# Gate and branch projections of a hybrid block written token-major, with a transpose of the merged result

## Chip, cores and metric

One core of one Trainium2 chip. The metric is the device time of one execution in microseconds, that of the only core; three runs of a kernel are made and their median is given.

## The reference

Two layers of a mixer and a feed-forward net on 256 tokens of width 1024, all in float32. Cut to what the change touches:

```python
proj = x @ w_in
gq, gk, gv, gg, glr, gz, mq, mk, mv, gl = jnp.split(proj, offsets, axis=-1)
a = gla_branch(gq, gk, gv, gg, glr, w_gate_up, b_gate, gla_norm_w) @ w_branch[0]
b = gmlp_branch(gz, gmlp_ln_g, gmlp_ln_b, gmlp_w_s, gmlp_b_s) @ w_branch[1]
c = moba_branch(mq, mk, mv, positions) @ w_branch[2]
ga, gb, gc = jnp.split(jax.nn.sigmoid(gl), N_BRANCH, axis=-1)
return (ga * a + gb * b + gc * c) @ w_out
```

`gl` has 3 x 1024 columns (the gates), each `w_branch` is 512 x 1024, `w_out` is 1024 x 1024. After it come a residual and a layer norm, then `square(relu(x @ w_ff1)) @ w_ff2` with 4096 hidden columns and a second layer norm.

## The kernel before

**Products.** A float32 product is made of three products of rounded operands: with x = hi + lo, each weight is split into `whi` (ScalarE, `split_hi`, L115) and `wlo` (VectorE, `split_lo`, L120), each activation likewise, and TensorE adds hi·hi, hi·lo and lo·hi in a PSUM bank. There are three ways to do so:

- `acc_s` (L281): the activation (128 tokens) is the stationary operand and the weight moves, three matmuls for each block of 128 inputs; with 512 weight columns that is 3 x 512 moving columns, and the result is token-major (tokens on the partitions).
- `acc_wide` (L265): the weight (128 columns) is stationary and the tokens move. One matmul with 512 moving columns takes `whi` against hi and lo side by side, one with 256 takes `wlo` against hi. The result is channel-major, in two halves of a bank that `fold` (L277) adds with a ScalarE copy and a VectorE add.
- `acc_w` (L255): the same with three matmuls of 256 moving columns, no fold.

A product of 1024 columns with all 256 tokens has the same number of moving columns in each of the three.

**Order of the work.** The program is a list of units (`add_unit`): each has TensorE work on one or two pieces of weight (512 KB each, loaded by the SyncE queue, SP), and often a `post` that empties its banks. The loop at L1061 goes through the units; at each it first advances the generators in `side` by one step (`advance`), then puts out the splits due there (`splits`), then the unit's matmuls, then its `post`. Pieces are split up to 7 units ahead (`LEAD`), in 9 buffers; the raw pieces go through 4 buffers (and 6 more early on), and a load is issued when `take_lo` has freed its buffer. All five queues work in this order; what an engine waits for holds up all that is behind it there. The PSUM banks are two rings of four, `pw` and `ps`.

**Units of a layer.** First `v` and `gv` (in layer 0 by `first_units`, L589: one piece of k = 0 for `v`, one for `gv`, then pieces of both for k = 1 to 7; the activations come in four pieces, split by `split_x` when the first unit that needs them is prepared), `u`, `gg`, the gates of branch b (`post_gl(1)`), the product of branch b (`branch_units`, L769, by `acc_w`), gk, gq, mq, mk, mv, the gates of a and c between the small matmuls of the attention (`moba_main`), the products of branches a and c, `w_out`, the layer norm, and the feed-forward units. Gates, u, gk, gq, mq, mk and `ff1` go through `acc_wide`; v, gv, gg, mv, `w_out` and `ff2` through `acc_s`.

**Gates and merge.** `gates` is one tile of 24 blocks of 128 channels x 256 tokens. `post_gl` folds a block; a later step applies the sigmoid in place. `post_bb`, `post_ba`, `post_bc` multiply a branch's block in its bank with its gate (VectorE); `post_ba` and `post_bc` add up the three on GpSimd (L815, L825). Since the sum is channel-major it is at once the stationary operand of `w_out`: `split` (L827) makes its hi (ScalarE) and lo (VectorE), block by block. `transpose_split` (L211), with four 128x128 transposes on TensorE, a ScalarE copy and a VectorE subtraction, turns token-major data and is used behind the layer norms.

Of the kernel before, what the change touches and what calls it, by code (L numbers as in the profile page):

```python
# [9 lines left out]
F32 = mybir.dt.float32  # L10
# [11 lines left out]
NT = 2  # L22
# [32 lines left out]
def block_kernel(ctx, tc, ins, out):  # L55
# [247 lines left out]
    def build_layer(l, xT):  # L303
# [285 lines left out]
        def first_units():  # L589

            blocks = [(0, piece(w_in[:, 0:1, C_V:C_V + 512], 1, 512)), (0, piece(w_in[:, 0:1, C_GV:C_GV + 512], 1, 512))]
            blocks += [(k, piece(w_in[:, k:k + 1, C_V:C_V + 1024], 1, 1024)) for k in range(1, 8)]
            heads = {0: 0, 2: 1, 3: 2, 5: 3}
            for n, (k, p) in enumerate(blocks):
# [3 lines left out]
                def pe(k=k, p=p, n=n):  # L598
                    for i, nm in enumerate(("v", "gv")):
                        if n < 2 and i != n:  # L600
                            continue
                        c0 = i * 512 if n > 1 else 0
# [6 lines left out]
                    for i, nm in enumerate(("v", "gv")):  # L609
                        if n < 2 and i != n:  # L610
                            continue
                        c0 = i * 512 if n > 1 else 0
# [135 lines left out]
        def post_gl(br):  # L748
            def post(m, p):
                if "G" not in st:  # L750
                    st["G"] = v3(sbt("G", 6144, "gates"), 24)
                G = st["G"]
                i = br * 8 + m
                fold(G[:, i], p)
                raw = st.setdefault("raw", [])
                raw.append(i)
                if m % 2 and (br == 1 or st.get("exps_done")):
                    def act():
                        while raw:
                            a = raw.pop(0)  # L760
                            nc.scalar.activation(G[:, a], G[:, a], AF.Sigmoid)
                        yield
                    side.append(act())
            return post

        st["glb_unit"] = len(units)
        w_units(C_GL + 1024, 8, post_gl(1))

        def branch_units(br, key, post):  # L769
            wb = ins["w_branch"][l][br].rearrange("(k p) c -> p k c", p=128)  # L770
            for j in range(4):
                b = w_pieces(wb, j * 256, 256, 4)[0]

                def pe(b=b, j=j):
                    for i in range(2):
                        st["pb", br, 2 * j + i] = pbank("pw", "pB")
                        acc_w(st["pb", br, 2 * j + i][:, :256], b, st[key], slice(i * 128, (i + 1) * 128), 0, True, True)

                def po(j=j):
                    for i in range(2):  # L780
                        post(2 * j + i, st["pb", br, 2 * j + i][:, :256])
                add_unit([b], pe, po)

        def post_bb(m, p):
            g = st["G"][:, 8 + m]
# [20 lines left out]
        w_units(C_GL, 8, post_gl(0))  # L806
        units[first_gl].start = lambda: side.append(moba_main())
        w_units(C_GL + 2048, 8, post_gl(2))


        def post_ba(m, p):
            G = st["G"]
            g = G[:, m]
            nc.vector.tensor_tensor(g, p, g, op=OP.mult)
            nc.gpsimd.tensor_tensor(G[:, 8 + m], G[:, 8 + m], g, op=OP.add)  # L815
# [4 lines left out]
        def post_bc(m, p):  # L820
            G = st["G"]
# [292 lines left out]
```

## Time and profile before

| | us |
|---|---|
| median of three runs (872.25 to 872.44) | 872.27 |
| the profiled execution | 872.83 |
| its span | 871.1 |
| TensorE (PE) matmuls busy | 860.2 (99%) |
| weight loads (PEld) busy | 751.4 (86%) |
| VectorE (DVE) busy | 617.7 (71%) |
| ScalarE (ACT) busy | 468.0 (54%) |
| GpSimd (POOL) busy | 59.5 (7%) |

Busy times are a share of the span; the profiled execution takes 1.7 us more than its span. A matmul's own duration overlaps that of the next, so what one costs is read from the distance between the starts of two, or from a run of many in the chain of work that ended last.

### The profile page before, as it was taken

How to read it: one execution, taken by the hardware profiler on the slowest of the kernel's cores; microseconds unless marked ns; L12 is line 12 of the kernel's file. 1: busy time of each engine (PE TensorE's matmuls, PEld its weight loads, DVE VectorE, ACT ScalarE, POOL GpSimd, SP SyncE). 2: the span in 40 equal slices, each digit the busy share in tenths (PEclk: the TensorE clock that was granted, in tenths of full speed). 3: DMA queues.
4: the chain of work that ended last, by engine and by line, in shares of the span. 5: the costliest groups of instructions: out<-in, count | busy, mean ns of one | idle time of the engine just before them, and what ended most of it. 6: DMA issues, size and time to landing. Idle time of an engine off the chain costs nothing.

```text
span 871.1 us, 13093 instructions
## 1 busy us (share of the span) xinstructions
PE 860.2 (99%) x5020; PEld 751.4 (86%) x5020; DVE 617.7 (71%) x949; ACT 468.0 (54%) x768; POOL 59.5 (7%) x73
## 2 busy tenths in 40 slices
PE   9999999999999999999999999999999999999996
PEld 7898887889989888888889898878898988888885
DVE  6779798666796666666777767958667856666665
ACT  6657663567445544445454756645744555444440
POOL 0010000102400000000000100010042000000001
PEclk9999999999999999999999999999999999999999
DMA  9577665346566655556655765544467465555531
GB/s 324 201 220 214 198 218 151 115 148 191 189 198 212 217 190 186 190 191 209 216 172 170 218 198 165 171 120 146 151 217 229 147 224 193 193 194 194 194 121 48
DMA packets 118718, 162.10 MB, mean 186 GB/s; under 512 B 5472, under 2 KB 100480, under 8 KB 118656
## 3 DMA queue, kind: packets, MB, share of 16 engines
q1 hardware_dynamic: 118512, 161.15, 57.8%
q8 instruction: 39, 0.64, 0.3%
q14 instruction: 23, 0.19, 0.1%
q10 hardware_dynamic: 144, 0.13, 0.0%
HBM read 160.21 MB, written 1.05 MB: 185 GB/s over the span
## 4 chain that ended last, share of the span: by engine, by line
PE 92%; DVE 3%; DMA 2%; ACT 1%; issue 1%; SPq 0%; DVEq 0%; ACTq 0%
PE acc L287 25%; PE pW L275 25%; PE pF L275 17%; PE pB L263 8%; PE pF L287 4%; PE pSmv L287 3%; DVE wlo L120 1%; PE pGG L287 1%; PE pSgv L287 1%; PE pSv L287 1%; PE pkv L457 1%; DMA xraw<-in_xT_dram 1%; DMA inv<-in_rope_inv_dram 1%; PE po L481 1%; PE pT L214 1%
## 5 line engine op out<-in xcount | busy, mean ns | idle before, releaser
L115 ACT CAST whi<-wraw 128x1024 fp32r<-128x1024 f32 (+1 forms) x281 | 283.3, 1039 | 132.2 <-DMA wraw<-in_w_ff_dram 63.2
L120 DVE TENSOR_TENSOR wlo<-wraw,whi 128x1024 fp32r<-128x1024 f32 (+1 forms) x281 | 334.7, 1226 | 18.1 <-ACT whi L115 17.8
L275 PE MATMUL pW<-actT,whi 128*128 128x512 f32 x704 | 248.3, 401 | 0.0
L275 PE MATMUL pW<-actT,wlo 128*128 128x256 f32 x704 | 183.3, 281 | 0.0
L287 PE MATMUL acc<-whi,h 128*128 128x512 f32 x512 | 163.4, 391 | 0.0
L275 PEld LDWEIGHTS pW<-actT,whi 128*128 128x128 f32 x704 | 128.1, 188 | 24.4
L275 PE MATMUL pF<-actT,whi 128*128 128x512 f32 x416 | 146.7, 397 | 0.0
L275 PEld LDWEIGHTS pW<-actT,wlo 128*128 128x128 f32 x704 | 132.9, 189 | 7.3 <-DVE wlo L120 0.2
L287 PEld LDWEIGHTS acc<-whi,h 128*128 128x128 f32 x512 | 96.2, 188 | 19.0
L275 PE MATMUL pF<-actT,wlo 128*128 128x256 f32 x416 | 108.4, 281 | 0.0
L287 PE MATMUL acc<-wlo,h 128*128 128x512 f32 x256 | 99.8, 390 | 0.0
L279 DVE TENSOR_TENSOR fr<-pF,fr 128x256 f32<-128x256 f32 x52 | 21.9, 424 | 102.0 <-ACT fr L278 102.0
L275 PEld LDWEIGHTS pF<-actT,whi 128*128 128x128 f32 x416 | 76.5, 188 | 15.4
L275 PEld LDWEIGHTS pF<-actT,wlo 128*128 128x128 f32 x416 | 78.5, 189 | 4.4
L287 PEld LDWEIGHTS acc<-wlo,h 128*128 128x128 f32 x256 | 48.1, 188 | 10.0
L278 ACT COPY fr<-pF 128x256 f32<-128x256 f32 x52 | 19.1, 372 | 59.4 <-PE pF L275 59.4
L209 POOL TENSOR_TENSOR mvar<-mvar,halfc 128x1 f32<-128x1 f32 x12 | 10.8, 904 | 443.1 <-DVE mvar L208 443.1
L287 PE MATMUL acc<-whi,actT 128*128 128x512 f32 x128 | 40.3, 391 | 0.0
L287 PE MATMUL pF<-whi,actT 128*128 128x256 f32 x192 | 36.6, 287 | 0.0
L279 DVE TENSOR_TENSOR gates<-pW,gates 128x256 f32<-128x256 f32 x48 | 19.5, 421 | 17.8 <-ACT gates L278 17.4
L278 ACT COPY gates<-pW 128x256 f32<-128x256 f32 x48 | 16.9, 370 | 27.3 <-PE pW L275 27.3
L946 ACT CAST h<-fr 128x256 fp32r<-128x256 f32 x52 | 19.3, 407 | 21.5 <-DVE fr L945 21.5
(234 smaller groups left out, 1238.6 us busy)
## 6 DMA issues: line engine op xcount, KB each, us to landing
wraw<-in_w_ff_dram SPq DMA_DIRECT2D x128, 512.0 KB, 4.9
wraw<-in_w_in_dram SPq DMA_DIRECT2D x104, 512.0 KB, 4.3
wraw<-in_w_branch_dram SPq DMA_DIRECT2D x24, 512.0 KB, 4.3
wraw<-in_w_out_dram SPq DMA_DIRECT2D x16, 512.0 KB, 3.3
wearly<-in_w_in_dram SPq DMA_DIRECT2D x7, 512.0 KB, 9.4
wraw<-in_w_in_dram SPq DMA_DIRECT2D x6, 396.0 KB, 4.4
lng<-in_ln_g_dram SPq DMA_DIRECT2D x4, 512.0 KB, 5.4
lnb<-in_ln_b_dram SPq DMA_DIRECT2D x4, 512.0 KB, 7.3
```

The source lines that it names most:

```text
L115: nc.scalar.copy(p.hi, p.raw)
L120: nc.vector.tensor_tensor(p.lo, p.raw, p.hi.bitcast(F32), op=OP.subtract)
L209: nc.gpsimd.tensor_tensor(dst, dst, half_c.to_broadcast([128, n]) if n > 1 else half_c, op=OP.pow)
L214: nc.tensor.transpose(p[:, k * 128:(k + 1) * 128], src[:, (half * 4 + k) * 128:(half * 4 + k + 1) * 128], ident)
L263: nc.tensor.matmul(o, w, a, start=start and i == 0 and j == 0, stop=stop and i == n - 1 and j == 2)
L275: nc.tensor.matmul(d, w, a, start=start and i == 0 and j == 0, stop=last and j == 1)
L278: nc.scalar.copy(dst, p[:, 256:])
L279: nc.vector.tensor_tensor(dst, p[:, :256], dst, op=OP.add)
L287: nc.tensor.matmul(o, a, w, start=start and j == 0, stop=stop and j == 2)
L457: nc.tensor.matmul(p[:, h * 128:(h + 1) * 128], kT4[rows, t, h, :], v4[rows, t, h, :], start=True, stop=True)
L481: nc.tensor.matmul(p[r, c], at4[:, t, h, r], v4[:, t, h, :], start=first and r.start == 0, stop=True)
L946: nc.scalar.copy(hi[:, i], rr[i])
```

## The change

Four edits:

1. **Gates** (`gl_units`, `half_units`): by `acc_s`, token-major, in two halves of 512 columns, each four units with one piece of two k (512 columns). The `post` of a half puts the sigmoid from the bank straight into `gates` for 128 x 512 at a time; the gates of a, which are ready before the exponentials of the attention are done, are copied first and get their sigmoid later. There is no fold.
2. **Branch products and merge** (`branch_units`): by `half_units` too, two units for each half, products on 128 x 512. The last addition is on VectorE, that of a stays on GpSimd. The sum is token-major and has to be turned: `turn` calls `transpose_split` for each token tile and half, two steps of `advance` after its `post`.
3. **`acc_wide`**: instead of wide and narrow in turn, all wide matmuls of a unit's k together and all narrow ones together (wide first, but narrow first in the unit that closes the bank). This holds for u, gk, gq, mq, mk and `ff1`, which stay channel-major.
4. **`first_units`**: the pieces of k = 1 for `v` and `gv` are apart, as those of k = 0 were, with 512 columns each, in the order v of k = 0 and 1, gv of k = 0 and 1. There is one unit more, the parameters' load moves from unit 3 to unit 5.

```diff
-        for i in range(n):
-            k = k0 + i
-            tr = [(o, p.hi[:, i, cs], both[:, k, :]), (o[:, :256], p.lo[:, i, cs], hi[:, k, :])]
-            last = stop and i == n - 1
-            for j, (d, w, a) in enumerate(tr[::-1] if last else tr):
-                nc.tensor.matmul(d, w, a, start=start and i == 0 and j == 0, stop=last and j == 1)
+        wide = [(o, p.hi[:, i, cs], both[:, k0 + i, :]) for i in range(n)]
+        narrow = [(o[:, :256], p.lo[:, i, cs], hi[:, k0 + i, :]) for i in range(n)]
+        tr = narrow + wide if stop else wide + narrow
+        for j, (d, w, a) in enumerate(tr):
+            nc.tensor.matmul(d, w, a, start=start and j == 0, stop=stop and j == len(tr) - 1)
...
-            blocks = [(0, piece(w_in[:, 0:1, C_V:C_V + 512], 1, 512)), (0, piece(w_in[:, 0:1, C_GV:C_GV + 512], 1, 512))]
-            blocks += [(k, piece(w_in[:, k:k + 1, C_V:C_V + 1024], 1, 1024)) for k in range(1, 8)]
-            heads = {0: 0, 2: 1, 3: 2, 5: 3}
+            blocks = [(k, piece(w_in[:, k:k + 1, c:c + 512], 1, 512)) for c in (C_V, C_GV) for k in (0, 1)]
+            blocks += [(k, piece(w_in[:, k:k + 1, C_V:C_V + 1024], 1, 1024)) for k in range(2, 8)]
+            heads = {0: 0, 1: 1, 4: 2, 6: 3}
...
+        def half_units(src, kt, xk, post):
+
+            for hf in range(2):
+                for k0 in range(0, kt, 2):
+                    b = piece(src(k0, hf * 512), 2, 512)
+
+                    def pe(b=b, k0=k0, hf=hf):
+                        x = xk()
+                        for t in range(NT):
+                            if k0 == 0:
+                                st["phalf", hf, t] = pbank("pw", "pH")
+                            for i in range(2):
+                                acc_s(st["phalf", hf, t], b, i, x, k0 + i, t, slice(0, 512), k0 + i == 0, k0 + i == kt - 1)
+
+                    def po(hf=hf):
+                        for t in range(NT):
+                            post(t, slice(hf * 512, (hf + 1) * 512), st["phalf", hf, t])
+                    add_unit([b], pe, po if k0 == kt - 2 else None)
...
+            def post(t, sl, p):
+                g = gates(br, t)[:, sl]
+                if br == 1 or st.get("exps_done"):
+                    nc.scalar.activation(g, p, AF.Sigmoid)
+                else:
+                    nc.scalar.copy(g, p)
+                    st.setdefault("raw", []).append(g)
...
-        def post_bc(m, p):
-            G = st["G"]
-            g = G[:, 16 + m]
-            hi, lo, _ = mT()
-            nc.vector.tensor_tensor(g, p, g, op=OP.mult)
-            nc.gpsimd.tensor_tensor(g, g, G[:, 8 + m], op=OP.add)
-
-            def split():
-                nc.scalar.copy(hi[:, m], g)
-                nc.vector.tensor_tensor(lo[:, m], g, hi[:, m].bitcast(F32), op=OP.subtract)
-                yield
-            side.append(split())
+        def post_bc(t, sl, p):
+            g = gates(2, t)[:, sl]
+            nc.vector.tensor_tensor(g, p, g, op=OP.mult)
+            nc.vector.tensor_tensor(g, g, gates(1, t)[:, sl], op=OP.add)
+
+            def turn():
+                yield
+                hi, lo, _ = mT()
+                transpose_split(gates(2, t), hi, lo, t, sl.start // 512)
+                yield
+            side.append(turn())
...
-    units[3].start = sts[0]["params"]
+    units[5].start = sts[0]["params"]
...
-    for n, c in ((0, 0), (2, 1), (3, 2), (5, 3)):
+    for n, c in ((0, 0), (1, 1), (4, 2), (6, 3)):
         load_more(n)
         load_xT(c)
```

**Where the order changes.** TensorE at the end of branch c (`pB` and `pH` are its banks, `ch` and `cl` the branch's hi and lo, `acc` the banks of `w_out`); before:

```order
L263 MATMUL pB<-ch,whi 128x256
L263 MATMUL pB<-cl,whi 128x256
L263 MATMUL pB<-ch,wlo 128x256
L287 MATMUL acc_2507<-whi,actT 128x512
L287 MATMUL acc_2507<-wlo,actT 128x512
L287 MATMUL acc_2507<-whi,actT 128x512
```

and in the change, ahead of the branch's last unit:

```order
L286 MATMUL pH<-whi,cl 128x512
L214 MATMUL pT<-ident,gates 128x128 x8
L286 MATMUL pH<-whi,ch 128x512
L286 MATMUL pH<-wlo,ch 128x512
L286 MATMUL pH<-whi,cl 128x512
```

and behind the first unit of `w_out`:

```order
L286 MATMUL acc_2172<-wlo,actT 128x512
L286 MATMUL acc_2172<-whi,actT 128x512
L214 MATMUL pT<-ident,gates 128x128 x8
L286 MATMUL acc_2201<-whi,actT 128x512
L286 MATMUL acc_2201<-wlo,actT 128x512
L286 MATMUL acc_2201<-whi,actT 128x512
```

Eight transposes stand ahead of the branch's last unit, and eight behind the first unit (12 matmuls) of `w_out`.

VectorE at the same place (`wlo` are the splits of coming weights); before, two of the four rounds of branch c:

```order
L120 TENSOR_TENSOR wlo<-wraw,whi 128x1024
L824 TENSOR_TENSOR gates<-pB,gates 128x256 x2
L829 TENSOR_TENSOR actT<-gates,actT 128x256 x2
L120 TENSOR_TENSOR wlo<-wraw,whi 128x1024
L824 TENSOR_TENSOR gates<-pB,gates 128x256 x2
L829 TENSOR_TENSOR actT<-gates,actT 128x256 x2
```

and in the change, both halves:

```order
L835 TENSOR_TENSOR gates<-pH,gates 128x512
L836 TENSOR_TENSOR gates<-gates 128x512
L835 TENSOR_TENSOR gates<-pH,gates 128x512
L836 TENSOR_TENSOR gates<-gates 128x512
L120 TENSOR_TENSOR wlo<-wraw,whi 128x1024 x2
L217 TENSOR_TENSOR actT<-pT,actT 128x4x128 x2
L120 TENSOR_TENSOR wlo<-wraw,whi 128x1024
L835 TENSOR_TENSOR gates<-pH,gates 128x512
L836 TENSOR_TENSOR gates<-gates 128x512
L835 TENSOR_TENSOR gates<-pH,gates 128x512
L836 TENSOR_TENSOR gates<-gates 128x512
L120 TENSOR_TENSOR wlo<-wraw,whi 128x1024
```

The products and sums of the second half stand behind the lo of the first half's turn (L217) and one split.

TensorE in the first units of u (`acc_wide`); before:

```order
L275 MATMUL pW<-actT,whi 128x512
L275 MATMUL pW<-actT,wlo 128x256
L275 MATMUL pW<-actT,whi 128x512
L275 MATMUL pW<-actT,wlo 128x256
L275 MATMUL pW<-actT,whi 128x512
L275 MATMUL pW<-actT,wlo 128x256
```

and in the change:

```order
L274 MATMUL pW<-actT,whi 128x512 x4
L274 MATMUL pW<-actT,wlo 128x256 x4
L274 MATMUL pW<-actT,whi 128x512 x4
L274 MATMUL pW<-actT,wlo 128x256 x8
L274 MATMUL pW<-actT,whi 128x512 x4
L274 MATMUL pW<-actT,wlo 128x256 x4
L274 MATMUL pW<-actT,whi 128x512 x8
```

The turns from narrow to wide become fewer: three in a round of 16 pairs.

## Rows read from the trace of the kernel before

**Rows 1.** Page, parts 1 and 2: busy time and share, and the clock in 40 slices.

```profile
span 871.1 us, 13093 instructions
...
PE 860.2 (99%) x5020; PEld 751.4 (86%) x5020; DVE 617.7 (71%) x949; ACT 468.0 (54%) x768; POOL 59.5 (7%) x73
...
PEclk9999999999999999999999999999999999999999
```

**Rows 2.** Waits of TensorE, the whole program: total us, times, longest.

```profile
PE pSv L614 <- DVE wlo L120: 1.1, 1, 1.1
...
PE plr L740 <- DVE gates L279: 0.8, 1, 0.8
```

**Rows 3.** Chain that ended last, TensorE's pieces: start us, us, instructions in a row.

```profile
95.57 28.16 PE pW L275 x160
...
209.47 23.02 PE pB L263 x192
...
280.15 5.63 PE pF L275 x32
285.78 5.44 PE acc L287 x24
...
432.27 0.87 PE pT L214 x8
...
441.34 1.01 PE pT L214 x8
...
447.83 5.44 PE pSv L287 x24
```

**Rows 4.** Timeline of TensorE, from branch c to w_out: start us, us, instruction.

```profile
232.21 0.28 PE L263 MATMUL pB<-ch,wlo 128*128 128x256 f32 x1
232.33 0.40 PE L287 MATMUL acc<-whi,actT 128*128 128x512 f32 x1
232.56 0.40 PE L287 MATMUL acc<-wlo,actT 128*128 128x512 f32 x1
...
233.49 0.62 PE L287 MATMUL acc<-whi,actT 128*128 128x512 f32 x2
```

**Rows 5.** Timeline of TensorE, layer 0's first matmuls.

```profile
5.89 0.63 PE L607 MATMUL pSv<-whi,actT 128*128 128x512 f32 x1
6.32 0.63 PE L608 MATMUL pSv<-whi,actT 128*128 128x512 f32 x1
...
10.41 0.39 PE L608 MATMUL pSgv<-whi,actT 128*128 128x512 f32 x1
11.87 0.73 PE L614 MATMUL pSv<-wlo,actT 128*128 128x512 f32 x2 [1.07 <-DVE wlo L120]
...
12.90 0.40 PE L607 MATMUL pSv<-whi,actT 128*128 128x512 f32 x1
```

**Rows 6.** Timeline of VectorE and ScalarE, layer 0's start.

```profile
9.99 0.69 DVE L984 TENSOR_TENSOR actT<-xraw,actT 128x512 fp32r<-128x512 f32 x1 [3.38 <-ACT actT L983]
10.59 2.42 DVE L120 TENSOR_TENSOR wlo<-wearly,whi 128x1024 fp32r<-128x1024 f32 x2
...
10.71 1.04 ACT L115 CAST whi<-wearly 128x1024 fp32r<-128x1024 f32 x1 [0.76 <-DMA wearly<-in_w_in_dram]
```

**Rows 7.** Timeline of TensorE, end of branch b's gates in layer 0.

```profile
73.63 0.28 PE L275 MATMUL pW<-actT,wlo 128*128 128x256 f32 x1
74.74 0.39 PE L740 MATMUL plr<-ident,lrs 128*16 128x128 f32 x2 [0.82 <-DVE gates L279]
```

**Rows 8.** VectorE's groups of instructions: shape and count | busy us, mean ns.

```profile
L120 DVE TENSOR_TENSOR wlo<-wraw,whi 128x1024 fp32r<-128x1024 f32 x272 | 327.0, 1237 | 18.1 <-ACT whi L115 17.8
...
L228 DVE SCALAR_TENSOR_TENSOR xr<-xr,acc 128x512 f32<-128x512 f32 x16 | 11.0, 686 | 11.8 <-PE acc L287 11.8
```

**Rows 9.** ScalarE's groups of instructions.

```profile
L115 ACT CAST whi<-wraw 128x1024 fp32r<-128x1024 f32 x272 | 276.7, 1048 | 131.7 <-DMA wraw<-in_w_ff_dram 63.2 <-DMA wraw<-in_w_in_dram 37.3 <-PE acc L287 11.9
```

**Rows 10.** Page, part 6: a load of w_out, us from issue to landing.

```profile
wraw<-in_w_out_dram SPq DMA_DIRECT2D x16, 512.0 KB, 3.3
```

More of the change, by code (lines that the diff above doesn't have):

```diff
@@ L599, in pe @@
                     for i, nm in enumerate(("v", "gv")):
-                        if n < 2 and i != n:
+                        if n < 4 and i != n // 2:
                             continue
-                        c0 = i * 512 if n > 1 else 0
+                        c0 = i * 512 if n > 3 else 0
                         for t in range(NT):
@@ L609, in pe @@
                     for i, nm in enumerate(("v", "gv")):
-                        if n < 2 and i != n:
+                        if n < 4 and i != n // 2:
                             continue
-                        c0 = i * 512 if n > 1 else 0
+                        c0 = i * 512 if n > 3 else 0
                         for t in range(NT):
@@ L746, in build_layer, with gates @@
         gg_units()
[L748 to L751, printed above, removed]
-                G = st["G"]
[L753 to L757, printed above, removed]
+        def gates(br, t):
+            if "G" not in st:
+                st["G"] = v3(sbt("G", 6144, "gates"), 6)
+            return st["G"][:, br * 2 + t]
@@ L758, in act, with gl_units @@
+        def gl_units(br):
+            c = C_GL + br * 1024
+            def post(t, sl, p):
[5 more added lines that the diff above has]
+                    st.setdefault("raw", []).append(g)
+                if t == 1 and st.get("raw") and st.get("exps_done"):
                     def act():
-                        while raw:
-                            a = raw.pop(0)
-                            nc.scalar.activation(G[:, a], G[:, a], AF.Sigmoid)
@@ L762, in act @@
-                        yield
+                        while st["raw"]:
+                            a = st["raw"].pop(0)
+                            nc.scalar.activation(a, a, AF.Sigmoid)
+                            yield
                     side.append(act())
-            return post
+            half_units(lambda k, c0: w_in[:, k:k + 2, c + c0:c + c0 + 512], 8, xT, post)
         st["glb_unit"] = len(units)
-        w_units(C_GL + 1024, 8, post_gl(1))
+        gl_units(1)
         def branch_units(br, key, post):
@@ L770, in branch_units @@
             wb = ins["w_branch"][l][br].rearrange("(k p) c -> p k c", p=128)
[L771 to L782, printed above, removed]
@@ L784, in post_bb @@
-        def post_bb(m, p):
-            g = st["G"][:, 8 + m]
+            half_units(lambda k, c0: wb[:, k:k + 2, c0:c0 + 512], 4, lambda: st[key], post)
+        def post_bb(t, sl, p):
+            g = gates(1, t)[:, sl]
             nc.vector.tensor_tensor(g, p, g, op=OP.mult)
@@ L1016, in block_kernel @@
         free = max(q.last for q in pieces[:n - SPLIT_BUFS + 1]) + 1 if n >= SPLIT_BUFS else -LEAD
-        s = max(prev + 1, free, p.first - (LEAD if n > 8 else 1))
+        s = max(prev + 1, free, p.first - (LEAD if n > 9 else 1))
         if count < 2 and max(prev, free) == prev and (p.first - s < 3 or p.first - s < LEAD - 1 and prev >= extra + 2):
@@ L1022, in block_kernel @@
         hi_at.setdefault(max(s, -1), []).append(p)
-        lo_at.setdefault(max(min(s + 1, p.first), s, -1) if n > 8 else max(s, -1), []).append(p)
+        lo_at.setdefault(max(min(s + 1, p.first), s, -1) if n > 9 else max(s, -1), []).append(p)
     loaded = [0]
```

13 lines of the change are left out of this document (6 added, 7 removed).

## The prediction

> **What bounds the kernel now.** I read the page's busy shares first, then the waits of TensorE, then the chain of work that ended last, and last the timeline where TensorE stands still. The reader is to see that TensorE's queue is the program's clock: PE is busy for 860.2 of 871.1 us, at a granted clock that the page prints as 9 (the 2.4 GHz level) in all 40 slices [rows 1]; behind its warm-up it waited for another engine only twice, 1.1 us for the low half of a weight in layer 0's start and 0.8 us at `plr` [rows 2]. VectorE (71%) and ScalarE (54%) are nowhere the bound for long [rows 1]. So an edit is worth what it takes out of TensorE's stream, plus those two waits, less new ones.
>
> A matmul's own duration says nothing here, since it overlaps with the next. The chain gives the pace [rows 3]: with 512 columns in `acc_s`, 24 in 5.44 us, 0.2267 us each (v, and `ff2` the same); with 256 in `acc_w`, 192 in 23.02 us, 0.1199 each; a pair of `acc_wide` (512 and 256 in turn), 80 in 28.16 us, 0.352 each, and 16 in 5.63 in `ff1`. A wide and two narrow ones have the same columns, but 2 x 0.1199 is 0.240 against 0.2267; a pair has one and a half times the columns of a wide one, and 1.5 x 0.2267 is 0.340 against 0.352. The stream pays for each matmul and not only for its columns.
>
> **Gates.** A layer has 3 x 8 blocks x 8 k = 192 pairs, the program 384: 135.2 us. In `acc_s` it is 3 branches x 2 halves x 2 token tiles x 8 k x 3 = 288 wide matmuls a layer, 576 in all: 130.6 us. **-4.6.** The small matmuls of the attention that lie between stay as they are.
>
> **Branch products.** 288 narrow ones a layer, 576 in all: 69.1 us; then 144 wide ones a layer, 288 in all: 65.3 us. **-3.8.** Both terms lie on the path whole, since TensorE is the path.
>
> [...]
>
> **Grouping.** What stays in `acc_wide` is 20 blocks x 8 k (u, gk, gq, mq, mk) and 208 pairs of `ff1` a layer, 736 pairs, 46 rounds of 16. A round takes 5.63 us; pure runs of either kind would make it 16 x 0.3466 = 5.55. So at most 0.08 us a round, 3.9 us in all, can be won. What a return from narrow to wide costs stands where branch c ends: the first five intervals of wide ones, 232.33 to 233.49, take 1.16 us where 5 x 0.2267 is 1.13 [rows 4], some 0.03 for one return behind a long narrow run. The new order has three returns a round: at 0.03 each nothing would be won. Blocks of four are shorter than those five intervals and I take half, 0.016 a return, 0.05 a round: **-1.6**, bounds 0 and -3.9.
>
> **Transposes.** Two layers x two halves x eight. Eight of them behind a layer norm take 0.87 us of the chain, once 1.01 [rows 3]: **+3.5**, up to 4.0. They could wait, too. For the second half VectorE has to do, behind the branch's last matmul, product and sum of the last tile, about 0.69 us each by the nearest row of this size [rows 8], 1.4 us; the cover is a `w_out` unit of 12 matmuls, 2.72 us. Ahead of that in its queue stand one split (1.24 us) and two lo of the first half's turn [rows 8], 2.6 us that can start 2.7 us earlier, when those transposes are out. It fits with about nothing to spare, so I put the wait at 0, with 0.6 us for each of the four as bound. What is queued behind waiting transposes is all of `w_out`; the banks behind the turn (ScalarE's hi, VectorE's lo) are wanted only two units later, 5.4 us.
>
> **First pieces.** TensorE's start 10.41 is followed by one at 11.87: 1.46 us where 0.23 is due [rows 5]. The cause is the order on VectorE: it splits the activations of k = 2 and 3 (9.99, when they had landed) ahead of the weights of k = 1 (10.59) [rows 6]. In the change the four small lo come first, so this wait goes. What is late next is k = 2: its weight's hi was made from 10.71 to 11.75 [rows 6], and TensorE began it at 12.90 [rows 5]. So 1.15 us at most; one load more now stands on SP's queue ahead of this weight, and I take **-0.9**, bounds 0 and -1.15. The parameters of the layer norm in the gMLP are asked for one piece later; they are wanted by VectorE alone, while TensorE has u ahead of it.
>
> **The wait at `plr`.** 73.63 to 74.74 is 1.11 us for a narrow matmul (0.12) [rows 7]: the next bank of the ring held a gate block whose fold was late on VectorE. With four banks for a whole branch's gates the bank in question was emptied by a sigmoid units before: **-1.0**, bounds 0 and -1.0.
>
> **At nothing:** the folds of the gates (gone), the sigmoids (now from the bank), the last additions (from GpSimd to VectorE), the loads of 2 x 512 instead of 4 x 256: all beside a TensorE that doesn't wait for them. If that cover went, it would be through the turn, below. There are as many weight pieces as before, but for one in the head.
>
> **Sum:** -4.6 - 3.8 - 1.6 + 3.5 - 0.9 - 1.0 = -8.4 us. The profiled execution took 872.83, so 864.4 for it; the median lies 0.56 lower, 872.27, and so I forecast **863.9**. What a measurement of this kernel can tell from no change is 0.2%, 1.74 us.
>
> **Rivals.**
> *The small terms fail:* grouping and head give nothing, `plr` waits for something else, the turns wait 0.6 us each: -8.4 + 1.6 + 0.9 + 1.0 + 2.4 + 0.5 = -2.0, at worst 870.3, still faster. For it: each rests on one or two rows. 14%.
> *Columns alone:* the pace goes with the columns, and the surplus of narrow ones is their surroundings'. Then gates, branches and grouping give nothing, and +3.5 - 0.9 - 1.0 = +1.6 makes 873.9, no change. Against it: 192 narrow ones in a row at 0.1199 and wide ones at 0.2267 in two places [rows 3]. 5%. [...]
> *The turn waits (slower):* VectorE works in order. If a split ahead of the second half's products waits for its weight of `w_out`, then load (3.3 us [rows 10]), hi (1.05 [rows 9]) and lo (1.24 [rows 8]) come before the transposes, and TensorE behind them stands still for up to 5.6 us a layer: 863.9 + 11.2 = 875.1. It decides from (8.4 + 1.7) / 2 = 5.1 us a layer. For it: ScalarE's casts do wait for loads (idle time before them in [rows 9]). Against it: splits run units ahead. 5%.
> *The clock falls (slower):* in the first microseconds 512 columns took 0.43 us (5.89 to 6.32), the pace of the 1.2 GHz level, though later 0.227 [rows 5]. If each of the four groups of transposes brought that back for the time it lasted at the start, some 6 us at half speed or 3 us each, 863.9 + 12 = 875.9. The Trainium skill says that transposes don't count as busy for the clock (TensorE: Matmul & The Clock Gate, Part 4: PE-mode transpose). Against it: behind the transposes at 441.34 wide matmuls go on at 0.2267 [rows 3], and no slice shows less than 9 [rows 1]. 3%.
>
> **How the numbers follow.** The forecast with its terms inside their bounds has 73%, from 872.27 - (4.6 + 3.8 + 3.9 - 3.5 + 1.15 + 1.0) = 861.3 to about 866.5. With better than half of the small-terms case, up to 868.5, that is 8 in 10: range 861.4 to 868.5. Faster by over 0.2%: 73 + 14 = 87%; within 0.2%: 5%; slower: 5 + 3 = 8%.
>
> **What would show it.** In the changed kernel's chain: `pH` matmuls at 0.2267 (a run of 24 in 5.44 us) in gates and branches; a round of 32 in `ff1` of 5.58 to 5.60 instead of 5.63; eight transposes of `gates` in some 0.87 us, twice a layer; no wait of TensorE at `plr`; k = 2 begun at about 12.0. It would be wrong if TensorE waited for VectorE at the transposes of `gates`, or if `pH` went slower than 0.2267.

## The result, and the profile after

The changed kernel takes 867.66 us (median of 4 runs, 867.23 to 867.99) where the kernel before takes 872.36: a ratio of 0.9942, 95% interval 0.9928 to 0.9956. The forecast was 863.9. The sign and the range held, but of the forecast gain of 8.4 us some 4.7 came. Run once more beside other kernels it took 867.25 us, with 873.38 for the kernel before, a ratio of 0.9929 (0.9915 to 0.9942).

The page, parts 1 and 2:

```profile
span 866.2 us, 12043 instructions
...
PE 854.9 (99%) x4572; PEld 729.0 (84%) x4572; DVE 605.1 (70%) x878; ACT 452.5 (52%) x697; POOL 43.3 (5%) x49
...
PEclk9999999999999999999999999999999999999998
```

TensorE is still the program's clock: 854.9 of 866.2 us, with 448 matmuls fewer than in [rows 1]. The granted clock stays at 9 up to the last slice, which is the program's end, and the trace gives 1.00 for the windows 224 to 226 and 230 to 233 us, where layer 0's groups of transposes stand: they cost none of it.

TensorE's waits (us in total, times, longest):

```profile
PE pSv L606 <- ACT whi L115: 1.1, 1, 1.1
PE warm L136 <- DVE warmt L131: 1.0, 1, 1.0
PE pT L214 <- DVE gates L836: 0.9, 2, 0.5
PE pSv L613 <- DVE wlo L120: 0.2, 1, 0.2
```

The line `warm` is the warm-up at the start, as before. Against [rows 2] the wait at `plr` and the one for the low half of k = 1 are gone. Two large ones are new: the one for the weights of k = 2 (`pSv`, line 606), and twice, once a layer, the one at the transposes of `gates`. A third, 0.2 us for the low half of k = 0 (line 613), is small.

The chain that ended last, pieces of TensorE and VectorE (start us, us, instructions in a row):

```profile
92.72 28.07 PE pW L274 x160
...
189.18 21.83 PE pH L286 x96
211.64 4.58 DVE wlo L120 x3
...
217.42 4.09 DVE wlo L120 x2
...
231.00 0.70 DVE gates L836
231.84 0.63 PE pT L214 x4
...
277.43 5.58 PE pF L274 x32
283.01 5.46 PE acc L286 x24
...
429.19 0.87 PE pT L214 x8
```

Set beside [rows 3]: where `pB` took 0.1199 us for 256 columns, `pH` takes 21.83 / 96 = 0.2274 for 512, in a run of 72 matmuls of c's gates and 24 of branch a. A round of `ff1` takes 5.58 instead of 5.63, but the 24 wide ones of `ff2` behind it 5.46 instead of 5.44. And from 211 to 231 us, in front of `w_out`, the chain runs through VectorE, which it never did there before.

The turn of the second half in TensorE's timeline:

```profile
230.77 0.60 PE L214 MATMUL pT<-ident,gates 128*128 128x128 f32 x4
231.84 0.63 PE L214 MATMUL pT<-ident,gates 128*128 128x128 f32 x4 [0.47 <-DVE gates L836]
```

Four transposes are out in 0.44 us; the second four begin 1.07 us behind the first. VectorE had only just made the second tile's sum (231.00 to 231.70 in the chain above).

Stages of TensorE read from its timeline, first matmul to first matmul, in us (in each cell layer 0, then layer 1):

| stage | before | after | differences |
|---|---|---|---|
| v, gv | 24.36, 22.82 | 24.06, 22.79 | -0.30, -0.03 |
| u, gg, gates of b | 48.54, 47.39 | 46.60, 46.60 | -1.94, -0.79 |
| branch b | 11.50, 11.50 | 10.88, 10.88 | -0.62, -0.62 |
| gk to mk | 51.38, 51.38 | 51.21, 51.21 | -0.17, -0.17 |
| gates of a and c | 51.88, 51.88 | 50.87, 50.87 | -1.01, -1.01 |
| branch a | 11.50, 11.50 | 10.88, 10.88 | -0.62, -0.62 |
| branch c | 11.52, 11.52 | 11.77, 11.77 | +0.25, +0.25 |
| w_out | 22.68, 22.68 | 24.25, 24.25 | +1.57, +1.57 |
| ff | 180.72, 179.59 | 180.37, 179.23 | -0.35, -0.36 |

The product of mv, between gk to mk and the gates of a and c, is left out (16.77 before, 16.81 after, in both layers). Where its code is the same, a stage repeats from kernel to kernel, mostly to 0.02 us and always to 0.1, so that an edit shows in its stage where the whole time, which moves by a microsecond between runs, hardly tells. Only layer 0's first two stages, where loads land now earlier and now later, differ between executions of the same code.

### The profile page after: what moved, and what is told of

It reads as the page before. It is cut to its first block, busy times and chain, and to the rows that moved or that the text cites. A ratio compares the mean times of both kernels' runs of the same rounds, so it can differ in the third digit from the quotient of the medians.

```text
span 866.2 us, 12043 instructions
## 1 busy us (share of the span) xinstructions
PE 854.9 (99%) x4572; PEld 729.0 (84%) x4572; DVE 605.1 (70%) x878; ACT 452.5 (52%) x697; POOL 43.3 (5%) x49
## 4 chain that ended last, share of the span: by engine, by line
PE 93%; DVE 5%; DMA 1%; issue 0%; SPq 0%; DVEq 0%; ACT 0%
PE acc L286 25%; PE pH L286 19%; PE pF L274 17%; PE pW L274 13%; PE pF L286 4%; DVE wlo L120 3%; PE pGG L286 3%; PE pSmv L286 3%; PE pSgv L286 1%; PE pSv L286 1%; DMA wearly<-in_w_in_dram 1%; PE pT L214 1%; PE pkv L456 1%; PE po L480 1%; DVE gates L835 1%; PE po L476 1%
## 5 line engine op out<-in xcount | busy, mean ns | idle before, releaser
L120 DVE TENSOR_TENSOR wlo<-wraw,whi 128x1024 fp32r<-128x1024 f32 (+2 forms) x282 | 338.4, 1237 | 31.9 <-ACT whi L115 31.4
L115 ACT CAST whi<-wraw 128x1024 fp32r<-128x1024 f32 (+2 forms) x282 | 284.0, 1038 | 145.0 <-DMA wraw<-in_w_ff_dram 61.9
L286 PE MATMUL pH<-whi,actT 128*128 128x512 f32 x384 | 124.4, 397 | 0.0
L274 PE MATMUL pW<-actT,whi 128*128 128x512 f32 x320 | 85.9, 395 | 0.0
L286 PEld LDWEIGHTS pH<-whi,actT 128*128 128x128 f32 x384 | 72.1, 188 | 14.9
L286 PE MATMUL pH<-wlo,actT 128*128 128x512 f32 x192 | 74.7, 389 | 0.0
L274 PEld LDWEIGHTS pW<-actT,whi 128*128 128x128 f32 x320 | 55.5, 188 | 8.7
L274 PE MATMUL pF<-actT,wlo 128*128 128x256 f32 x416 | 61.8, 280 | 0.0
L274 PEld LDWEIGHTS pW<-actT,wlo 128*128 128x128 f32 x320 | 46.5, 189 | 5.5
L274 PE MATMUL pW<-actT,wlo 128*128 128x256 f32 x320 | 48.7, 282 | 0.0
```

The lines of the kernel that those rows point to most:

```text
L115: nc.scalar.copy(p.hi, p.raw)
L120: nc.vector.tensor_tensor(p.lo, p.raw, p.hi.bitcast(F32), op=OP.subtract)
L274: nc.tensor.matmul(d, w, a, start=start and j == 0, stop=stop and j == len(tr) - 1)
L286: nc.tensor.matmul(o, a, w, start=start and j == 0, stop=stop and j == 2)
```

## The experiments

Ratios are to the kernel before, run beside each; spans and stages come from the profiled execution. The kernel before took 872.80 us beside some of these kernels and 873.38 or 873.36 beside the others, so medians a few tenths of a microsecond apart say nothing by themselves.

| kernel | median us | ratio, 95% | span | v, gv (layer 0) | u, gg, gates of b (layer 0) | w_out |
|---|---|---|---|---|---|---|
| changed, again | 867.25 | 0.9929 (0.9915 to 0.9942) | 865.5 | 23.37 | 46.60 | 24.25 |
| turn later | 866.18 | 0.9924 (0.9912 to 0.9937) | 864.4 | 23.50 | 46.60 | 23.58 |
| additions on VectorE | 866.56 | 0.9927 (0.9915 to 0.9940) | 864.8 | 23.76 | 46.60 | 23.58 |
| no transposes | 862.37 | 0.9882 (0.9867 to 0.9897) | 860.2 | 23.10 | 46.60 | 22.65 |
| old first pieces | 868.67 | 0.9953 (0.9941 to 0.9966) | 866.9 | 24.17 | 47.00 | 24.25 |
| old order in `acc_wide` | 868.27 | 0.9940 (0.9927 to 0.9952) | 866.3 | 23.33 | 46.65 | 24.25 |
| before + new order | 872.30 | 0.9987 (0.9979 to 0.9996) | 870.3 | 23.61 | 49.50 | 22.71 |
| before + late lo of x | 872.41 | 0.9988 (0.9979 to 0.9997) | 869.8 | 23.39 | 48.23 | 22.68 |
| before + small ones | 878.92 | 1.0064 (1.0048 to 1.0079) | 877.2 | 24.42 | 51.00 | 22.68 |
| changed + small ones | 875.25 | 1.0022 (1.0013 to 1.0031) | 873.7 | 23.92 | 50.41 | 24.25 |
| old pieces, new order of splits, additions on VectorE | 867.10 | 0.9927 (0.9914 to 0.9939) | 864.8 | 23.06 | 46.99 | 23.58 |
| k = 2 in halves, additions on VectorE | 867.38 | 0.9937 (0.9924 to 0.9949) | 865.6 | 23.70 | 47.36 | 23.58 |

### The wait at the turn

First theory: VectorE is late at the second half's turn and nowhere else. One more unit of `w_out` goes ahead of that turn:

```diff
+                if sl.start:
+                    yield
```

> The changed kernel, with the turn (transposes) of the second half put one unit of w_out, 12 matmuls or 2.72 us, later. Theory: TensorE stands still at the first transposes of that half because VectorE is late there by 0.5 to 0.9 us a layer, and only there; one unit more of cover takes it away: -1.3 us against the changed kernel (866.4 for 867.7), and the trace shows no wait of TensorE at the turn. Rival: VectorE's lateness is no matter of when the turn is asked for (it has too much work there altogether), or what stands at the turn is the transposes' own price: 0 us, and the wait shows up again at the turn or at w_out behind it, which starts later for lack of the split merged result.

Chain of this kernel, TensorE around that turn:

```profile
227.70 5.45 PE acc L286 x24
233.15 0.87 PE pT L214 x8
234.02 13.65 PE acc L286 x60
```

The eight transposes now go in one piece of 0.87 us, no wait at `pT` is left in the list of waits, and `w_out` takes 23.58 instead of 24.25 in both layers: -1.34 us. The theory holds. (The median came out 1.1 to 1.5 us lower, by which of the two measurements of the changed kernel it is compared with; the two ratios overlap, and it is the stage that shows it.)

Why VectorE is late was the second question. In the window 205 to 222 us of the changed kernel, VectorE's group of weight splits (busy us, mean ns of one), and GpSimd's timeline:

```profile
L120 DVE TENSOR_TENSOR wlo<-wraw,whi 128x1024 fp32r<-128x1024 f32 x6 | 10.0, 1702 | 4.7 <-ACT whi L115 4.7
```

```profile
210.44 3.56 POOL L828 TENSOR_TENSOR gates<-gates 128x512 f32<-128x512 f32 x2 [35.10 <-DVE gates L827]
216.90 3.53 POOL L828 TENSOR_TENSOR gates<-gates 128x512 f32<-128x512 f32 x2 [2.90 <-DVE gates L827]
```

A split takes 1702 ns here and 1237 on the whole program's mean [rows 8]. The 1702 is a mean of two kinds: in the trace three of the six take 1.21 to 1.23 us, as elsewhere, and the three that began while GpSimd was adding 1.93 to 2.32; of the four additions two take 1.3 and the two that began during a split 2.20 and 2.28. One of each:

```profile
211.80 2.20 POOL L828 TENSOR_TENSOR gates<-gates 128x512 f32<-128x512 f32 x1
212.77 2.31 DVE L120 TENSOR_TENSOR wlo<-wraw,whi 128x1024 fp32r<-128x1024 f32 x1
```

The addition ends at 214.00, 1.14 us behind the end of the split ahead of it (211.64 to 212.86), and the split shown ends at 215.08, 1.08 us behind the end of that addition: each looks like an instruction that did its work when the other was done. So the additions went to VectorE:

```diff
-            nc.gpsimd.tensor_tensor(s, s, g, op=OP.add)
+            nc.vector.tensor_tensor(s, s, g, op=OP.add)
```

> The changed kernel, with the additions of branch a's products made by VectorE instead of GpSimd (four of 128x512 a layer). Theory: while GpSimd adds, VectorE's splits of 1024 columns go from 1.24 us to 1.5 to 2.1 us, and this is why VectorE comes late to the turn; with the additions on VectorE (some 0.7 us each) the splits take 1.24 us again, the wait at the turn goes or halves: -0.6 to -1.3 us. Rival: VectorE simply has too much to do ahead of the turn, and 4 x 0.7 us more a layer make it later: the wait at the turn stays or grows, 0 to +2 us.

The same group of this kernel, same window:

```profile
L120 DVE TENSOR_TENSOR wlo<-wraw,whi 128x1024 fp32r<-128x1024 f32 x6 | 7.1, 1220 | 4.7 <-ACT whi L115 4.7
```

The six splits cost 2.9 us less, the four additions 2.8 more, and 0.7 of that falls into time in which VectorE had stood waiting for a product of branch a. The wait at the turn is gone from the list, `w_out` is at 23.58 in both layers. So the additions of GpSimd held VectorE up. The Trainium skill says so (SBUF — State Buffer, Who interferes with whom): an instruction of VectorE with two SBUF inputs contends with an instruction of GpSimd that reads SBUF. The trace agrees: 1.93 to 2.32 us against 1.22 for a split, and each of the slow ones ends 1.08 us behind the end of an addition. The forecast had the row of the splits and not the neighbour, though the trace of the kernel before shows the pair, with additions of 256 columns (0.74 us when alone there):

```profile
218.63 1.65 POOL L815 TENSOR_TENSOR gates<-gates 128x256 f32<-128x256 f32 x1 [0.53 <-DVE gates L814]
219.60 1.76 DVE L120 TENSOR_TENSOR wlo<-wraw,whi 128x1024 fp32r<-128x1024 f32 x1
```

Third, what the transposes themselves cost. The merged result goes into `w_out` as it lies:

```diff
-                transpose_split(gates(2, t), hi, lo, t, sl.start // 512)
+                half = sl.start // 512
+                to = (slice(None), slice(half * 4, half * 4 + 4), slice(t * 128, (t + 1) * 128))
+                g = v3(gates(2, t)[:, sl], 4)
+                nc.scalar.copy(hi[to], g)
+                nc.vector.tensor_tensor(lo[to], g, hi[to].bitcast(F32), op=OP.subtract)
```

> The changed kernel without the turning of the merged result: its hi and lo are taken from the token-major tile as it lies, so 32 transposes are left out of the program and the merged result goes untransposed into w_out. Theory: the transposes cost their own 3.5 us of TensorE's stream and the wait of VectorE at the second half's turn another 1.3: -4.9 us, 862.8. Rival 1: the wait has to do with VectorE's work only, and w_out waits for the halves' hi and lo instead: -3.5 us, 864.2. Rival 2: the transposes also slow the stream behind them (the matmuls behind a small one come late, or the clock falls): -6 us or more.

Chain of this kernel, the same place:

```profile
188.15 38.13 PE pH L286 x168
226.28 19.04 PE acc L286 x84
```

From the gates of c over branches a and c to `w_out` TensorE goes through without a stop. Branch c falls from 11.77 to 10.88 and `w_out` from 24.25 to 22.65, 2.49 us a layer, 5.0 in the program: 1.34 the wait, 3.6 the transposes. The theory's 4.9 holds; the medians differ by 4.9 to 5.3.

### The head

The first profile after shows what stands in the place of the wait that went (TensorE's timeline, then ScalarE's):

```profile
10.78 0.61 PE L613 MATMUL pSgv<-wlo,actT 128*128 128x512 f32 x2
12.54 0.50 PE L606 MATMUL pSv<-whi,actT 128*128 128x512 f32 x1 [1.14 <-ACT whi L115]
```

```profile
11.44 1.04 ACT L115 CAST whi<-wearly 128x1024 fp32r<-128x1024 f32 x1 [0.69 <-DMA wearly<-in_w_in_dram]
```

In [rows 6] the same cast began at 10.71: with the smaller pieces its load landed 0.7 us later in this execution. My theory was that the head had given nothing. The old first pieces were put back into the changed kernel:

```diff
-            blocks = [(k, piece(w_in[:, k:k + 1, c:c + 512], 1, 512)) for c in (C_V, C_GV) for k in (0, 1)]
-            blocks += [(k, piece(w_in[:, k:k + 1, C_V:C_V + 1024], 1, 1024)) for k in range(2, 8)]
-            heads = {0: 0, 1: 1, 4: 2, 6: 3}
+            blocks = [(0, piece(w_in[:, 0:1, C_V:C_V + 512], 1, 512)), (0, piece(w_in[:, 0:1, C_GV:C_GV + 512], 1, 512))]
+            blocks += [(k, piece(w_in[:, k:k + 1, C_V:C_V + 1024], 1, 1024)) for k in range(1, 8)]
+            heads = {0: 0, 2: 1, 3: 2, 5: 3}
...
```

> The changed kernel with the first pieces of the weights as before (one of 1024 columns for k = 1 instead of two of 512). Theory: the smaller pieces took away one wait in the head (1.2 us behind VectorE) and brought another of 1.1 us (k = 2, whose weight now lands 0.7 us later), so they are worth next to nothing: 0 to +0.4 us. The forecast had them worth 0.9: +0.9 us, 868.6, is the rival.

TensorE's waits of this kernel:

```profile
PE pSv L613 <- DVE wlo L120: 1.1, 1, 1.1
...
PE pW L274 <- DVE wlo L120: 0.2, 1, 0.2
```

868.67 us is 1.0 to 1.4 above the two medians of the changed kernel, though the intervals of the ratios overlap with the first. Beside it ran "turn later" and "additions on VectorE", with the new pieces; with the 1.34 us of the turn added they would take 867.5 and 867.9, 0.8 to 1.2 less than this kernel. So the theory falls, and the forecast's 0.9 is met. The old wait is back, and a small one in the first unit of u beside it: that stage takes 47.00 instead of 46.60, and this 0.4 is part of the 0.8 to 1.2. Then the changed kernel again:

> The changed kernel itself once more, as a yardstick on the same chip for the runs beside it and to see how far its head varies. Theory: TensorE's wait for the weights of k = 2 depends on when their load lands, and in the profiles of three kernels with the same head this wait came out at 0.4 to 0.8 us against 1.1 in the changed kernel's first profile, so that one was on the late side: 867.3 to 867.9 us, with a wait of 0.3 to 1.1 us for k = 2. The wait at the turn is not subject to that: 0.9 to 1.0 us again in the list of waits. Rival: the load of k = 2 always lands late with the smaller first pieces: a wait of 1.1 us again.

Its waits, and the cast of k = 2:

```profile
PE pT L214 <- DVE gates L836: 1.0, 2, 0.5
PE pSv L606 <- ACT whi L115: 0.4, 1, 0.4
```

```profile
10.68 1.05 ACT L115 CAST whi<-wearly 128x1024 fp32r<-128x1024 f32 x1 [0.81 <-DMA wearly<-in_w_in_dram]
```

The same code, and the load has landed 0.76 us earlier: the wait is 0.4 instead of 1.1, the one at the turn as it was. One profile had caught a late load, and I had read it as the effect of the pieces. Over the seven profiles with the new pieces as in the change (after, and six experiments) v and gv take 23.10 to 24.06, 23.6 in the mean; over the four with the old pieces and the old order of splits 23.61 to 24.42, 24.1 in the mean: 0.6 apart, and the ranges overlap.

The wait that the smaller pieces remove was one of VectorE's order, by the forecast. Then the order alone will do, in the kernel before:

```diff
-                    p.pre = lambda c=heads[n]: split_x(c)
+                    p.pre, p.pre_lo = lambda c=heads[n]: split_x(c), lambda c=heads[n]: split_x(c, True)
...
-        nc.scalar.copy(hi[:, k0:k1], src)
-        nc.vector.tensor_tensor(lo[:, k0:k1], src, hi[:, k0:k1].bitcast(F32), op=OP.subtract)
+        if low:
+            nc.vector.tensor_tensor(lo[:, k0:k1], src, hi[:, k0:k1].bitcast(F32), op=OP.subtract)
+        else:
+            nc.scalar.copy(hi[:, k0:k1], src)
```

> The kernel before with one thing altered: VectorE splits the activations of k = 2 and 3 (lo) only ahead of the lo of the weight that needs them, no longer ahead of the weights of k = 1. Pieces and loads stay as they were. Theory: the wait of 1.1 us for the low half of k = 1 is one of order on VectorE alone; without it k = 2 starts when its hi is there, 11.75 us or a little later instead of 12.90: -0.8 to -1.1 us, and no smaller pieces are needed for it. Rival: the low half of k = 1 waits for its own load and hi (8.4 to 9.5 us) and VectorE is behind altogether, or the activations' lo is then what is late at k = 2: 0 to -0.4 us.

TensorE's timeline of this kernel, the low half of k = 1 and the start of k = 2:

```profile
11.14 0.61 PE L616 MATMUL pSgv<-wlo,actT 128*128 128x512 f32 x2
11.80 0.50 PE L609 MATMUL pSv<-whi,actT 128*128 128x512 f32 x1
```

k = 2 starts at 11.80 instead of 12.90 [rows 5] and the median falls by 0.97 us, as the theory had it. Both cures end at the same bound, the cast of k = 2 (10.70 to 11.75 us in this kernel). Now three edits together: the changed kernel with the old first pieces, this late split, and the additions on VectorE:

> The changed kernel with the first pieces as before, the activations' lo of k = 2 and 3 split only when its weight needs it, and branch a's additions on VectorE. Theory: the wait in the head was one of VectorE's order, so a new order does what the smaller pieces do, and the additions on VectorE take the wait at the turn away: no wait at the turn, the stage of v and gv at 23.4 us (the changed kernel showed 23.4 and 24.1), 866.0 us or a ratio of 0.992. Rival: the smaller pieces are needed as well, since with them the low half of k = 1 comes earlier: v and gv at 24.0 or more and a wait of VectorE's in the units behind it, 867 us.

v and gv take 23.06, as the theory had it, in a stage that varies by a microsecond; a wait of 0.2 us in u remains, as the rival had it (stage 46.99). The median, 867.10, is the rival's figure; the ratio, 0.9927, is that of the kernel with the smaller pieces and the additions on VectorE. So the smaller pieces showed no gain over the order alone, within intervals of some 0.1% to either side. And going further with them, halves for k = 2 as well, beside the additions on VectorE:

```diff
-            blocks = [(k, piece(w_in[:, k:k + 1, c:c + 512], 1, 512)) for c in (C_V, C_GV) for k in (0, 1)]
-            blocks += [(k, piece(w_in[:, k:k + 1, C_V:C_V + 1024], 1, 1024)) for k in range(2, 8)]
+            blocks = [(k, piece(w_in[:, k:k + 1, c:c + 512], 1, 512)) for ks in ((0, 1), (2,)) for c in (C_V, C_GV) for k in ks]
+            blocks += [(k, piece(w_in[:, k:k + 1, C_V:C_V + 1024], 1, 1024)) for k in range(3, 8)]
...
```

> The changed kernel with branch a's additions on VectorE and the weights of k = 2 loaded and split in two halves of 512 columns as well. Theory: with smaller first pieces the head is bound by the load of k = 2 and the cast of its 1024 columns behind it (1.05 us); half a piece lands half its load earlier and is cast in some 0.5 us, so TensorE's wait of 0.4 to 1.1 us for k = 2 goes: -0.4 to -0.9 us against the changed kernel with those additions, 865.8 to 866.1, ratio 0.992 or less. Rival: one piece more delays all the loads behind it and k = 3 is late instead: 0 or +0.3 us.

TensorE's waits:

```profile
PE pSv L613 <- DVE wlo L120: 0.9, 1, 0.9
PE pW L274 <- DVE wlo L120: 0.5, 1, 0.5
```

and VectorE's timeline ahead of the first of them (TensorE's wait ends at 16.75):

```profile
14.33 1.23 DVE L996 TENSOR_TENSOR actT<-xraw,actT 128x1024 fp32r<-128x1024 f32 x1 [2.29 <-ACT actT L995]
15.47 4.63 DVE L120 TENSOR_TENSOR wlo<-wraw,whi 128x1024 fp32r<-128x1024 f32 x4
```

The theory falls: the wait for k = 2 is gone, and two of VectorE's stand behind it, together 1.4 us. k = 3 is late, as the rival had it, but not by its load: its hi was made by 13.02 us, and VectorE stood still for 2.29 us because the lo of the activations of k = 4 and later is ahead of the lo of that weight in its queue. That is the order of [rows 6] over again, one step on. v and gv take as long as without the halves (23.70 for 23.76) and u takes 0.8 us longer, more than the rival's 0.3.

### The order in `acc_wide`

The old order put back into the changed kernel:

```diff
-        wide = [(o, p.hi[:, i, cs], both[:, k0 + i, :]) for i in range(n)]
-        narrow = [(o[:, :256], p.lo[:, i, cs], hi[:, k0 + i, :]) for i in range(n)]
-        tr = narrow + wide if stop else wide + narrow
...
+            tr = [(o, p.hi[:, i, cs], both[:, k, :]), (o[:, :256], p.lo[:, i, cs], hi[:, k, :])]
...
```

> The changed kernel with the old order in acc_wide (512 and 256 columns in turn), all else as changed. Theory: the grouping is worth 0.05 us in a round of ff1 (16 pairs), less 0.02 in the ff2 round behind it, and some 0.8 us a layer in the other pairs... taken together +1.2 us. Forecast of record: +1.6 us (46 rounds of 16 pairs at 0.035 each). Rival: pure runs pay the full 0.08 a round: +3.9; or nothing: 0.

Its chain in `ff`:

```profile
276.71 5.63 PE pF L275 x32
282.33 5.44 PE acc L287 x24
```

868.27 us beside 867.25: +1.0, nearest to the theory's 1.2, and by the stages 0.47 a layer (0.36 of it in ff, the rest in gk to mk and u). Of the 0.05 us that a round of `ff1` gains, the 24 wide ones behind it give 0.02 back. In the kernel before, the new order alone (the diff above, its signs turned round):

> The kernel before with the new order in acc_wide alone. Here the gates are still pairs as well, 1120 pairs in all or 70 rounds of 16. Theory: what a pair gains does not depend on its surroundings: -1.2 us x 1120/736 = -1.8 us. By the term of the forecast (0.035 a round of 16): -2.4. Rival: with both orders a return from narrow to wide costs the same and there are three such returns in a round of the new order: 0 us.

-1.1 us, less than all but the rival's zero. Layer 1's stages sum to -0.65 (mv counted, which takes 0.04 more), which would be -1.3 for both layers; in layer 0 a wait grew:

```profile
PE plr L739 <- DVE gates L278: 1.4, 1, 1.4
```

It was 0.8 [rows 2]. TensorE came to `plr` 0.3 us earlier (v and gv were 0.75 shorter in this execution, and a wait of 0.2 in u gave some of it back) and VectorE 0.3 later: a gain ahead of a wait is given back in the wait. That the change could keep its own because it took that wait away as well is likely, but was not tried by itself.

### What the gates lost

The gates of b gained what was forecast, those of a and c a third less. Between them lie the attention's small matmuls, eight groups a layer. Four transposes into a bank that nobody reads went ahead of each of b's eight units of gates, in the kernel before and in the changed one:

```diff
+    def small_ones():
+        p = pbank("ps", "few")
+        for q in range(4):
+            nc.tensor.transpose(p[:, q * 128:(q + 1) * 128], ident, ident)
```

> The kernel before with 16 interruptions added: ahead of each of the eight units of branch b's gates (pairs of 512 and 256 columns), in both layers, TensorE makes four transposes of 128x128 into a bank that nobody reads. Beside the next run it measures what a stream of pairs pays for being interrupted by small matmuls. Theory: four small ones cost 4 x 0.109 us and the stream loses little more: 16 x 0.47 = +7.5 us. This number is a reference for the next run; of the theories, only the difference of the two tells.

> The changed kernel with the same 16 interruptions, ahead of the eight units of branch b's gates, now 12 matmuls of 512 columns each. Theory: wide matmuls that come behind small ones take 0.231 to 0.236 us instead of 0.227 for the next ten or so, so an interruption costs a wide stream some 0.065 us more than one of pairs: the stage of branch b's gates grows by 16 x 0.065 = 1.0 us more in the program than in the run of pairs (+8.6 against +7.5). This is where the gates' missing 1.1 us would be, since the attention's small matmuls interrupt the gates of a and c eight times a layer. Rival: both streams pay the same, and the missing gain lies in the small matmuls themselves: equal growth within 0.3 us.

The chains of the four kernels at the gates of b in layer 1, in the order before, before with the small ones, after, after with them:

```profile
483.36 19.71 PE pW L275 x112
```

```profile
486.04 0.44 PE few L214 x4
486.47 2.78 PE pW L280 x16
...
489.69 2.83 PE pW L280 x16
```

```profile
480.18 19.07 PE pH L286 x84
```

```profile
483.77 0.44 PE few L214 x4
484.21 2.77 PE pH L291 x12
...
487.42 2.77 PE pH L291 x12
```

Undisturbed, 8 pairs take 19.71 / 7 = 2.82 us; behind small ones seven such stretches take 2.78 to 2.83, 2.81 in the mean: nothing lost. Undisturbed, 12 wide ones take 19.07 / 7 = 2.72; behind small ones 2.76 or 2.77 all seven times: 0.04 lost for each interruption. The stage grew by 3.45 us in layer 1 of the one and 3.84 of the other, 0.4 a layer apart or 0.8 in the program: less than the theory's 1.0, well above the rival's 0.3. (The first kernel as a whole grew by 5.6 and not by 7.5: in layer 0 its stage grew by only 2.5, since the wait at `plr` vanished behind the added work. The second grew by 8.0, where 8.6 had been expected.)

The change's own gates of a and c show the same, chain of after:

```profile
164.18 2.77 PE pH L286 x12
...
168.38 5.49 PE pH L286 x24
```

2.77 for 12 and 5.49 for 24, where 2.72 and 5.44 were reckoned with.

## Why the prediction was right, and where it was off

The forecast was 863.9 and the kernel takes 867.66. That lies in the range, but beyond 866.5, up to which the prediction saw its terms inside their bounds: what held was the part of the range that had been added for half of the rival *The small terms fail*. Nearly all misses went the same way. Both signs by which the prediction said that it would be wrong came, too: TensorE waits for VectorE at the transposes of `gates`, and `pH` goes slower than 0.2267 in the gates of a and c.

Its step **Sum** by terms, forecast and found (us, the program):

| term | forecast | found | from |
|---|---|---|---|
| gates | -4.6 | -3.5 | stages a layer: -0.74 (46.65 with the old order, for 47.39) and -1.01 |
| branch products | -3.8 | -3.8 | stages, branch c without transposes 10.88 |
| grouping | -1.6 | -0.9 to -1.0 | old order put back |
| transposes | +3.5 | +3.6 | transposes left out, less the wait |
| wait at the turn | 0 | +1.3 | turn later; additions on VectorE |
| first pieces | -0.9 | -0.3 in the first profile, -0.6 in the mean of v and gv; about -1.0 with old pieces put back | profiles; old pieces put back |
| `plr` | -1.0 | -1.15 | -1.94 of layer 0's stage less layer 1's -0.79 |

With -0.3 for the head the column sums to -4.8; the two profiles' spans differ by 4.9. Putting the old pieces back costs more than the change gained by them, since in the changed kernel they also bring a wait in u (0.4), which the kernel before did not have.

- **The method held.** TensorE's stream is the program's clock, and the pace of an instruction taken from a run of its kind in the chain, 0.2267 for 512 columns, 0.1199 for 256, gave the branch products and the gates of b to a tenth of a microsecond. That 512 columns are cheaper than twice 256, the claim against which the rival *columns alone* stood, is shown: branch b went from 11.50 to 10.88 with the same columns, 48 matmuls of 0.2267. The change swaps the operands' roles at the same time, which could be the reason instead; but the kernel before has matmuls of 256 columns in `acc_s`, too, and they go at 5.75 / 48 = 0.1198:

```profile
255.17 5.75 PE pF L287 x48
```

- **Transposes** were right: eight in 0.87 us, and the clock stayed.
- **The failed step is the wait at the turn.** The text reckoned VectorE's queue with splits of 1.24 us and found that it fits "with about nothing to spare"; then it took the favourable end of the bound, 0 of 0.6. It let the lo of the first half's turn start when those transposes are out. They were out at 225.23 us, and VectorE came to that lo at 226.49, since the splits ahead take 2.9 us more beside GpSimd's additions than without them; the lack showed as 0.67 a layer. The turn of the first half did not wait. The bound was right, the value taken was not: with no slack and one neighbour left out, the upper end was the likelier.
- **Gates, mis-sized.** Both paces were taken from undisturbed runs, and the text let the attention's small matmuls "stay as they are". They do, but they set back the wide stream behind them: in the stretch of a and c 512 columns take 0.2282 (49.30 us for the 216 up to and with the first branch matmuls) and a pair before took 0.3505 (44.86 us for 128), where 0.2267 and 0.352 were put in. That is 192 x 0.0015 + 128 x 0.0015 = 0.5 a layer, nearly all of the missing 1.1 of the program. The larger part is the slower wide stream, which the added small ones show; the rest, that the pairs before were a little quicker in this stretch than 0.352, is read from the chain alone.
- **Grouping, mis-sized.** Half of the return cost, 0.05 us a round, was right for `ff1` but for the 0.02 that the wide ones behind it give back; and in the 10 other rounds a layer only 0.01 came.
- **First pieces, right in the mechanism.** The wait of VectorE's order went, and what was late next was k = 2, as said; it began at 12.54 and 11.78 in two profiles, for 12.0 forecast. The size of 0.9 is met only with the 0.4 in u, which the forecast didn't have; the stage of v and gv alone gave 0.6 in the mean.
- **`plr`, right** in size; that it was the free bank was not tried by itself.

A version with the same result that beats the changed kernel beyond its interval wasn't found. "Turn later" and "additions on VectorE", which take the wait at the turn away, have spans of 864.4 and 864.8 (changed: 865.5 and 866.2), and either is the one to keep; both at once was not tried.

## What to carry to other kernels

When one engine's stream is the program, take each instruction's pace from a run of its own kind in the chain, then ask what lies between: a pace read from an undisturbed run is too good for a stretch that other instructions cut up. Where a new dependence is said to fit without slack, look at what another engine does at the same time, in the trace that is at hand, and take the pessimistic end. And don't read a load's landing time from one profile: repeat the same kernel first.

## What had not been expected of the hardware

- A split of 128x1024 on VectorE that began during an addition of 128x512 on GpSimd took 1.93 to 2.32 us instead of 1.22, and an addition that began during a split 2.20 or 2.28 instead of 1.3.
- Behind a group of small matmuls a run of 12 with 512 columns takes 2.77 us instead of 2.72. A stream of 512 and 256 in turn takes 2.81 for 16, disturbed or not. A pair of them takes 0.352 where its columns would take 0.340 at the wide pace. That this is the same surcharge paid all the time is a guess: no run here shows it.
